# A list-scheduled decoder step: other prices for DMA loads in the planner, another lift for attention

## The chip, the cores and the metric

The kernel runs on one core of a Trainium2 chip. What counts is the device time of one execution in microseconds; of the kernel before, three runs gave a median of 1370.7 us (1368.8 to 1371.14). The engines are TensorE (PE, its weight loads PEld), VectorE (DVE), ScalarE (ACT), GpSimd (POOL) and SyncE (SP), which issues all DMAs here.

## The reference

Two layers of a hybrid decoder are applied to a prompt of 512 tokens and to 8 decoding sequences of 4 tokens, 544 columns in all, with a model width of 1024. In each layer:

```
mod = silu(c) @ w_mod + b_mod                  # 6 x 1024 columns: shift, scale, gate, twice
h = rmsnorm(x) * (1 + sc1) + sh1
z = h @ w_in                                   # q, k, v | u (SSM) | a, g (convolution)
o_attn = windowed attention with rope and sinks (8 q heads, 2 kv heads, window 128)
o_ssm  = S5 diagonal state space on u, gelu, sigmoid gate
o_conv = GLU(a, g) -> causal depthwise conv, width 31 -> LayerNorm -> silu
x = x + g1 * (concat(o_attn, o_ssm, o_conv) @ w_out)
h2 = rmsnorm(x) * (1 + sc2) + sh2
x = x + g2 * ((silu(h2 @ w_gate) * (h2 @ w_up)) @ w_down)     # inner width 2816
```

and a final RMSNorm follows. Keys, values, SSM states and convolution history are returned too.

## The kernel before, in words

**Work and tiles.** Activations lie transposed: 128 channels in the partitions, 544 tokens in two halves of 272. Each large product is split in three: weights and activations are each written as a high and a low part (hi, lo in a type of TensorE's fast path), and `mm3` multiplies hi by hi, hi by lo and lo by hi. `split` (line 543) loads a 128 x 1024 weight block of 512 KB into a tile raw, of which there are two (NRAW, line 39), writes its hi part on ScalarE or VectorE and its lo part on POOL or VectorE; of hi and lo there are four each (NW). `prefetch` (line 552) asks for blocks two ahead of their use. `mtiles` (line 567) issues the stream of matmuls.

**Modulation.** `mod_group` (line 582) computes columns of mod: per block of w_mod a load into raw (the same two buffers) and 8 matmuls of 128 x 256 into the PSUM tile mod. After the start, three groups of layer 0 (one of layer 1) run up to and in its mixing stage; the layer's last group and, in layer 0, four of the next layer run between the feed-forward matmuls (`mod_turn`, line 1399).

**The middle of a layer.** STEPS (line 206) lists in program order the projections (columns by COLS: q, v, u for the SSM, a and g for the convolution), `s5`, `attention` (line 1196), `convolve` (line 1165) for two halves of the channels, and the convolution's norm. The SSM and the convolution rearrange their data by a store to DRAM and a gather from it (tiles d_s).

**What sets the order.** Nothing in that program order is final. The program is traced once into a list of operations; `_schedule` (line 212) plans them, and the plan alone decides each engine's order, the buffer of each tile and, where two engines can do an operation, the engine. It is a list schedule: it walks through a modelled time, and whenever an engine is free it takes, among the operations whose inputs the model believes ready, the one with the highest rank. A rank is the longest modelled path to the end of the program (line 294), plus a lift (line 297) that the code sets by hand: `order.lift` is ULIFT = 150e3 in the SSM, CLIFT = 0 in the convolution, QLIFT in attention, LIFT = 150e3 or MLIFT = 700e3 for modulation blocks, in nanoseconds of rank.

Durations of operations come from `_cost`. A DMA is modelled in three parts. It begins 1100 ns after its issue or when the modelled bus is free (line 414); it holds the bus for its bytes over a rate (`lat`, line 232); and its consumer may start a hop later (`hop`, line 284), which for a DMA is one number for any consumer. `lat` and `hop` also enter the ranks. On the chip each engine runs its own list strictly in order and waits by semaphores: an operation planned too early holds up all behind it on its engine.

Of the kernel before, what the change touches and what calls it, by code (L numbers as in the profile page):

```python
# [136 lines left out]
def _box(ap):  # L137
    dims = [tuple(d) for d in ap.ap]
    pitch = max(dims[0][0], 1)
    p0, f0 = divmod(ap.offset, pitch)  # L140
    return p0, p0 + dims[0][1], f0, f0 + 1 + sum(s * (n - 1) for s, n in dims[1:])
# [58 lines left out]
FLIFT = 20e3  # L200
MT0, MT1 = 0, 1
MODS = (2, 3, 4), (4,), (1, 0, 2, 3)
PLIFT, ULIFT, CLIFT, QLIFT = (0.0, 0.0), 150e3, 0.0, 50e3
COLS = (("a0", "g0", "u0", "u1", "q4", "v0", "q0", "q1", "q2", "q3", "a1", "g1"),
        ("u0", "u1", "q4", "a0", "g0", "v0", "q0", "q1", "q2", "q3", "a1", "g1"))
STEPS = (((0, 1, 2), "taps", (3,), "c0", (4,), (5,), (6,), (7,), (8,), (9,), "s5", "attn", (10, 11), "c1", "norm"),
# [5 lines left out]
def _schedule(order, tags):  # L212
# [10 lines left out]
    lat = [0.0] * N  # L223
# [4 lines left out]
    for i, (opt, outs, ins, _, st, _, gl) in enumerate(ops):  # L228
        eng, fn = opt[0]
        if fn == "dma_start":  # L230
            a = max(outs[0], ins[0], key=lambda v: v.size() if v.space != bass.MemoryType.DRAM else 0)
            lat[i] = outs[0].size() * 4 / 360.0
        for kind, aps in ((0, ins), (1, outs)):
            for ap in aps:
                name = ap.tensor.name
                if ap.space == bass.MemoryType.DRAM and name not in tags:
                    continue
                if name in tags:
                    uses.setdefault(name, set()).add(i)
                    if name not in first:  # L240
                        first[name] = i
                box = _box(ap) if ap.space != bass.MemoryType.DRAM else (0, 1, 0, 1)
                h = hist.setdefault(name, [])
                keep = []
                for e in h:
                    b, w, j = e
                    hit = b[0] < box[1] and box[0] < b[1] and b[2] < box[3] and box[2] < b[3]
                    if hit and (w or kind) and j != i:
                        dep[i].add(j)
                    inside = kind and box[0] <= b[0] and b[1] <= box[1] and box[2] <= b[2] and b[3] <= box[3]  # L250
                    if not (inside and j != i):
                        keep.append(e)
                keep.append((box, kind, i))
                hist[name] = keep
        if eng == "PE":
            j = banks.get(outs[0].tensor.name)
            if j is not None:
                dep[i].add(j)
            banks[outs[0].tensor.name] = i
        if st:  # L260
            if last_stream is not None:
                follow[last_stream] = i
            last_stream = i
        if gl is not None:
            runs.setdefault(gl, []).append(i)
# [18 lines left out]
    def hop(j, i):  # L284
        a, b = ops[j][0][0], ops[i][0][0]
        if a[1] == "dma_start":
            return 960.0
        if a[0] == b[0]:
            return 0.0 if a[0] == "PE" else 127.0
        return 280.0 if b[0] == "PE" else 197.0 if "PE" in a or b[0] == "Pool" else 147.0  # L290

    rank = [0.0] * N
    for i in range(N - 1, -1, -1):
        rank[i] = cost[i][0] + lat[i] + max((hop(i, s) + rank[s] for s in succ[i]), default=0.0)
        if i in follow:
            rank[i] = max(rank[i], cost[i][0] + rank[follow[i]])
# [36 lines left out]
    while done < N:  # L333
        progress = True
        while progress:
            progress = False
            for e in engs:
# [28 lines left out]
                _, r, i, p = best  # L366
# [61 lines left out]
        while ev and ev[0][0] <= now:  # L428
            t, i, kind, *more = heapq.heappop(ev)
            if kind == 0:  # L430
                for o, _ in ops[i][0]:
                    bisect.insort(pool[o], (-rank[i], i))
            elif kind == 3:
                n, j = more[0]
                free[tags[n][0]].append(held[n])
                freed_by[tags[n][0], held[n]] = j
            elif kind == 1:
                for n in touch[i]:
                    left[n] -= 1
                    if left[n] == 0:  # L440
                        serial += 1
                        heapq.heappush(ev, (now + 200.0, serial, 3, (n, i)))
                for s in succ[i]:
                    if t + hop(i, s) >= arrive[s]:
                        arrive[s] = t + hop(i, s)
                        last_dep[s] = i
                    wait[s] -= 1
                    if wait[s] == 0:
                        heapq.heappush(ev, (max(arrive[s], now), s, 0))
# [1217 lines left out]
def _ordered(program):  # L1667

    trace = _Order()
    try:  # L1670
        program(trace)
    except _Traced:
        pass
    return program(_Order(_schedule(trace, trace.tiles)))
# [19 lines left out]
```

## Time and profile before

| | |
|---|---|
| median of 3 runs | 1370.7 us |
| the profiled execution | 1367.83 us, of it 1365.6 us from the first to the last instruction |
| TensorE busy | 1304.9 us (96%), 10440 matmuls |
| VectorE, ScalarE, POOL busy | 728.3, 435.0, 360.0 us |
| mean granted TensorE clock | 0.978 |
| read from HBM | 164.22 MB |

The stages of the profiled execution: up to about 45 us the start (x, modulation and SSM parameters), then layer 0's mixing to about 240, its output projection and feed-forward part to about 715, layer 1's mixing to about 905, and its feed-forward part to the end. All compute instructions are recorded under line 111, that of the helper, so that tiles and stretches tell them apart, not lines. A busy TensorE says only that a matmul was in it; the granted clock beside it says at which of two speeds (1.2 and 2.4 GHz, written as 0.5 and 1.0).

### The profile page before, as it was taken

Reading aid. Unit: us, or ns where it says so; the run is one execution under the profiler, and the core shown is the slowest. Engines: PE = TensorE matmul, PEld = TensorE weight load, DVE = VectorE, ACT = ScalarE, POOL = GpSimd, SP = SyncE. Lnnn points to the kernel's source line nnn. Section 1 sums busy time; section 2 is a strip of 40 time slices with the busy share of each in tenths; the row PEclk is TensorE's granted clock in tenths of the full one; section 3 lists DMA queues with packets and bytes.
Section 4 is the critical chain, followed back from the end, with each engine's and each line's share of the span. In section 5 each row is a group of like instructions: output and inputs, shape, how many; then the busy total and the mean of one; then the engine's idle time right before and its main releaser. Section 6 shows DMA issues by size and latency. Waiting matters only on the chain.

```text
span 1365.6 us, 25552 instructions
## 1 busy us (share of the span) xinstructions
PE 1304.9 (96%) x10440; PEld 1221.9 (89%) x10440; DVE 728.3 (53%) x1695; ACT 435.0 (32%) x929; POOL 360.0 (26%) x439
## 2 busy tenths in 40 slices
PE   7999799999999999999999999998999999999997
PEld 6987658998898888999999976898999999999997
DVE  6867975766743323334448977377534433433443
ACT  4452472442221112222226455134322211222232
POOL 7763110354422001222102521112122200222211
PEclk9999899999999999999998999999999999999998
DMA  9656474315545545222223384323352222222321
GB/s 334 214 161 197 130 252 127 117 59 174 170 142 170 171 133 166 85 93 93 94 83 98 116 261 129 120 71 105 109 154 84 83 97 94 78 78 93 97 75 66
DMA packets 79653, 176.57 MB, mean 129 GB/s; under 512 B 22768, under 2 KB 40496, under 8 KB 79536
## 3 DMA queue, kind: packets, MB, share of 16 engines
q1 hardware_dynamic: 79536, 174.94, 39.9%
q8 instruction: 82, 1.34, 0.4%
q14 instruction: 35, 0.29, 0.1%
HBM read 164.22 MB, written 10.70 MB: 128 GB/s over the span
## 4 chain that ended last, share of the span: by engine, by line
PE 64%; DMA 12%; DVE 6%; ACT 2%; issue 1%; POOL 1%; SPq 0%; DVEq 0%; ACTq 0%; POOLq 0%
PE ps_s L111 61%; DMA raw_s<-w_mod 7%; DVE pg_s L111 4%; PE mod_s L111 2%; DMA raw_s<-w_up 2%; ACT hi_s L111 1%; POOL lo_s L111 1%; DMA pg_s<-d_s 1%; DVE lo_s L111 1%; DMA raw_s<-w_down 1%; DMA d_s<-pg_s 1%; DMA raw_s<-w_gate 1%; DVE cr_s L111 1%; ACT pg_s L111 0%; DVE cs_s L111 0%
## 5 line engine op out<-in xcount | busy, mean ns | idle before, releaser
L111 PE MATMUL ps_s<-pg_s,hi_s 128*128 128x272 f32 x5504 | 1060.0, 291 | 4.5 <-ACT pg_s L111 2.6
L111 PEld LDWEIGHTS ps_s<-pg_s,hi_s 128*128 128x128 f32 x5504 | 870.1, 189 | 25.6 <-issue 16.9
L111 PE MATMUL ps_s<-pg_s,lo_s 128*128 128x272 f32 x2752 | 794.3, 290 | 0.4 <-POOL lo_s L111 0.3
L111 PEld LDWEIGHTS ps_s<-pg_s,lo_s 128*128 128x128 f32 x2752 | 519.9, 189 | 10.3 <-issue 9.2
L111 POOL TENSOR_TENSOR lo_s<-raw_s,hi_s 128x1024 fp32r<-128x1024 f32 x74 | 212.1, 2869 | 572.4 <-DVE hi_s L111 418.7
L111 ACT ACTIVATE hi_s<-raw_s 128x1024 fp32r<-128x1024 f32 x129 | 136.4, 1060 | 371.1 <-PE ps_s L111 278.1
L111 DVE TENSOR_TENSOR lo_s<-raw_s,hi_s 128x1024 fp32r<-128x1024 f32 x98 | 123.1, 1256 | 85.1 <-ACT hi_s L111 84.3
L111 PE MATMUL ps_s<-pg_s,pg_s 128*128 128x104 f32 (+10 forms) x864 | 131.6, 331 | 12.0 <-DVE pg_s L111 4.8
L111 DVE TENSOR_TENSOR pg_s<-w_s,pg_s 128x272 fp32r<-128x272 f32 x143 | 112.4, 791 | 43.0 <-ACT pg_s L111 42.6
L111 PEld LDWEIGHTS ps_s<-pg_s,pg_s 128*128 128x128 f32 (+4 forms) x864 | 105.3, 195 | 33.4 <-issue 13.4
L111 ACT ACTIVATE w_s<-ps_s 128x272 f32<-128x272 f32 (+1 forms) x172 | 66.9, 389 | 177.9 <-PE ps_s L111 173.3
L111 DVE CAST hi_s<-raw_s 128x1024 fp32r<-128x1024 f32 x43 | 29.8, 693 | 149.0 <-PE ps_s L111 145.8
L111 DVE SCALAR_TENSOR_TENSOR x<-ps_s,modT_s,x 128x272 f32<-128x272 f32 (+1 forms) x96 | 45.7, 481 | 106.0 <-PE ps_s L111 105.9
L111 ACT ACTIVATE pg_s<-w_s 128x272 fp32r<-128x272 f32 x147 | 61.5, 427 | 88.8 <-DVE w_s L111 85.3
L111 DVE TENSOR_TENSOR w_s<-w_s,ps_s 128x272 f32<-128x272 f32 x88 | 38.1, 433 | 85.7 <-ACT w_s L111 75.6
L111 PE MATMUL mod_s<-raw_s,silu_c 128*32 128x256 f32 x640 | 51.0, 394 | 22.1 <-DMA raw_s<-w_mod 20.9
L111 POOL TENSOR_TENSOR acc_s<-acc_s,w_s 128x272 f32<-128x272 f32 x9 | 9.5, 1059 | 192.3 <-ACT w_s L111 140.8
L111 ACT ACTIVATE pg_s<-ps_s 128x512 f32<-128x512 f32 (+11 forms) x100 | 34.4, 378 | 50.2 <-PE ps_s L111 44.7
L111 ACT ACTIVATE w_s<-x 128x272 f32<-128x272 f32 x70 | 29.0, 426 | 63.1 <-DVE x L111 58.7
L111 PEld LDWEIGHTS mod_s<-raw_s,silu_c 128*32 128x32 f32 x640 | 13.0, 108 | 38.5 <-DMA raw_s<-w_mod 28.1
L111 DVE TENSOR_TENSOR acc_s<-acc_s,w_s 128x272 f32<-128x272 f32 x60 | 35.4, 605 | 20.6 <-ACT w_s L111 20.5
L111 ACT ACTIVATE w_s<-w_s,modT_s,gain_s 128x272 f32<-128x272 f32 (+1 forms) x64 | 35.8, 591 | 18.7 <-DVE w_s L111 15.5
(140 smaller groups left out, 787.9 us busy)
## 6 DMA issues: line engine op xcount, KB each, us to landing
raw_s<-w_mod SPq DMA_DIRECT2D x80, 512.0 KB, 3.8
raw_s<-w_gate SPq DMA_DIRECT2D x44, 512.0 KB, 3.5
raw_s<-w_up SPq DMA_DIRECT2D x44, 512.0 KB, 3.9
raw_s<-w_down SPq DMA_DIRECT2D x44, 512.0 KB, 3.5
raw_s<-w_in SPq DMA_DIRECT2D x24, 512.0 KB, 4.7
pg_s<-cwt SPq DMA_DIRECT2D x20, 512.0 KB, 6.7
pg_s<-w_mod SPq DMA_DIRECT2D x32, 256.0 KB, 6.0
raw_s<-w_out SPq DMA_DIRECT2D x16, 512.0 KB, 3.5
```

Source lines behind the costliest of these rows:

```text
L111: r = real(*a, **k)
```

## The change

The rate in `lat` goes from 360 to 320 bytes per nanosecond; the hop behind a DMA goes from 960 to 1500 ns, with separate names for a consumer on TensorE and elsewhere, both 1500; attention's lift goes from 50e3 to 100e3. The set of operations, their shapes and the DMAs stay; the plan, and with it each engine's order, buffers and choices, is made anew.

```diff
-PLIFT, ULIFT, CLIFT, QLIFT = (0.0, 0.0), 150e3, 0.0, 50e3
+DRATE, DHOP, DPE = 320.0, 1500.0, 1500.0
+PLIFT, ULIFT, CLIFT, QLIFT = (0.0, 0.0), 150e3, 0.0, 100e3
...
         if fn == "dma_start":
             a = max(outs[0], ins[0], key=lambda v: v.size() if v.space != bass.MemoryType.DRAM else 0)
-            lat[i] = outs[0].size() * 4 / 360.0
+            lat[i] = outs[0].size() * 4 / DRATE
...
         a, b = ops[j][0][0], ops[i][0][0]
         if a[1] == "dma_start":
-            return 960.0
+            return DPE if b[0] == "PE" else DHOP
```

## Rows read from the trace of the kernel before

**Rows 1.** The page's first part: busy time, share of the span, instructions.
```profile
PE 1304.9 (96%) x10440; PEld 1221.9 (89%) x10440; DVE 728.3 (53%) x1695; ACT 435.0 (32%) x929; POOL 360.0 (26%) x439
```

**Rows 2.** TensorE's waits, whole span: us in total, times, longest.
```profile
PE mod_s L111 <- DMA raw_s<-w_mod: 20.9, 29, 2.5
PE ps_s L111 <- ACT pg_s L111: 8.2, 5, 2.9
PE ps_s L111 <- DVE pg_s L111: 6.7, 6, 3.5
...
PE ps_s L111 <- DMA pg_s<-d_s: 1.4, 2, 0.8
```

**Rows 3.** The same in 100:140, then 280:380 (two rows), 380:530 and 945:1010.
```profile
PE mod_s L111 <- DMA raw_s<-w_mod: 2.9, 2, 1.6
...
PE mod_s L111 <- DMA raw_s<-w_mod: 3.8, 8, 0.7
PE ps_s L111 <- POOL lo_s L111: 0.3, 1, 0.3
...
PE mod_s L111 <- DMA raw_s<-w_mod: 4.5, 8, 1.0
...
PE mod_s L111 <- DMA raw_s<-w_mod: 1.7, 5, 0.6
```

**Rows 4.** DMA issues (KB each, median us to landing), then all landings of raw.
```profile
raw_s<-w_mod SPq DMA_DIRECT2D x80, 512.0 KB, 3.8
...
DMA to landing us min/median/max: 3.3/3.8/9.8
```

**Rows 5.** Chain of waits, feed-forward of layer 0: start us, us, what.
```profile
331.25 4.22 DMA raw_s<-w_mod
...
335.52 0.68 PE mod_s L111 x8
...
343.33 4.67 DMA raw_s<-w_mod
...
348.04 0.68 PE mod_s L111 x8
```

**Rows 6.** TensorE in order of time around 120 us; in brackets idle before.
```profile
118.97 0.64 PE L111 MATMUL mod_s<-raw_s,silu_c 128*32 128x256 f32 x8 [1.56 <-DMA raw_s<-w_mod]
...
124.94 0.64 PE L111 MATMUL mod_s<-raw_s,silu_c 128*32 128x256 f32 x8 [1.38 <-DMA raw_s<-w_mod]
```

**Rows 7.** TensorE and ScalarE in order of time, before each feed-forward part.
```profile
272.74 0.73 ACT L111 ACTIVATE pg_s<-w_s 128x272 fp32r<-128x272 f32 x2
273.56 0.68 PE L111 MATMUL mod_s<-raw_s,silu_c 128*32 128x256 f32 x8 [2.55 <-DMA raw_s<-w_mod]
...
943.40 1.08 PE L111 MATMUL mod_s<-raw_s,silu_c 128*32 128x256 f32 x8 [2.42 <-DMA raw_s<-w_mod]
944.28 0.73 ACT L111 ACTIVATE pg_s<-w_s 128x272 fp32r<-128x272 f32 x2
```

**Rows 8.** Windows: length, busy us by engine, PEclk, DMA share, GB/s.
```profile
270.00:280.00 10.00, 7.45 (x43) 6.83 (x42) 8.87 (x32) 8.53 (x18) 4.08 (x6) 0.70 0.49 157
940.00:950.00 10.00, 7.44 (x39) 6.53 (x40) 8.57 (x20) 7.22 (x18) 3.27 (x2) 0.66 0.46 158
```

**Rows 9.** The same view of the start; PE busy is the second number.
```profile
10.00:40.00 30.00, 26.42 (x353) 20.40 (x351) 22.87 (x100) 16.62 (x37) 22.80 (x66) 1.00 1.08 369
```

**Rows 10.** Windows and TensorE's longest wait in layer 0's mixing stage (140:175, 140:210).
```profile
140.00:175.00 35.00, 27.08 (x196) 20.83 (x197) 31.68 (x117) 19.13 (x57) 6.85 (x8) 0.85 0.44 132
...
PE ps_s L111 <- DVE pg_s L111: 3.5, 1, 3.5
```

**Rows 11.** SP in order of time, end of layer 1's mixing; issues with landing.
```profile
862.37 0.38 SPq L111 DMA_DIRECT2D d_s<-pg_s  x1
...
866.70 0.33 SPq L111 DMA_DIRECT2D pg_s<-d_s  x1
...
pg_s<-d_s SPq DMA_DIRECT2D x4, 432.0 KB, 5.2
```

## Prediction

> **What bounds the kernel now.** I read the page first: TensorE is busy for 1304.9 of 1365.6 us, and the instructions are the same afterwards, so only the 60.7 us without a matmul and the stretches at the lower clock can be won [rows 1]. TensorE's waits come next: the largest entry, 20.9 us in 29 waits, is the modulation product (tile mod) standing for its load of w_mod into raw; waits for VectorE and ScalarE results (8.2, 6.7 and smaller ones) are spread over the layer's middle [rows 2]. Then the same view by stretch: 3.8 + 4.5 + 1.7 = 10.0 us of the 20.9, in 21 waits of about half a microsecond, lie in the feed-forward stretches 280 to 530 and 945 to 1010 us, and 2.9 us in 100 to 140 [rows 3]. The rest is two waits of 2.55 and 2.42 us [rows 7] and four of 0.75 us on average (20.9 - 10.0 - 2.9 - 5.0 = 3.0, 29 - 21 - 2 - 2 = 4).
>
> **Why they wait, and the load's price.** TensorE runs its list in order. The planner puts the product of a w_mod block (LIFT or MLIFT, ahead of nearly all else) where it believes the block arrives. It prices a 512 KB load (524288 bytes) at 1100 ns to start, 524288/360 = 1456 ns on the bus and 960 ns to the consumer: 3.52 us. After the change it is 1100 + 524288/320 + 1500 = 1100 + 1638 + 1500 = 4.24 us, 0.72 us more, and 0.18 us more for each further load that the planned bus has ahead of it. The trace has 3.8 us to landing in the median for w_mod, 3.3 at least and 9.8 at most over all raw loads [rows 4]; from issue to matmul, in the chain of waits, 331.25 to 335.52 is 4.27 us and 343.33 to 348.04 is 4.71 [rows 5]. The old price is 0.75 and 1.19 us short there, the new one 0.03 and 0.47.
>
> The Trainium skill (DMA: Bandwidth & Descriptors, section Anatomy of one DMA — SWDGE (gpsimd) path) puts a DMA issued by GpSimd (here SP issues) at about 2.0 us plus its bytes at 436 GB/s, an estimate of 3.2 us for such a load; by it 3.52 was dear already and dearer prices win nothing, the first rival's result. The trace disagrees: 3.2 lies under even the shortest landing, 3.3 [rows 4].
>
> **The change part by part.** All durations are of the profiled execution: 1365.6 us of span, 1367.8 us of its own time, 2.9 us under the median of 1370.7.
>
> *Feed-forward stretches.* A wait shorter than 0.72 us ends if the product merely moves back 0.72 us behind matmuls that are ready. Most of the 21 waits are (the longest are 0.7, 1.0 and 0.6 by stretch, the mean is 10.0/21 = 0.48), and what stands behind them is ready: in 280 to 380 us the feed-forward matmuls themselves wait only 0.3 us [rows 3]. So up to 9.7 of 10.0 us go. What is late next is raw itself: two buffers serve weights and w_mod, and the chain there goes load, ScalarE, VectorE or POOL, next load, and the next w_mod load of the chain goes out at 343.33, 12.1 us after the one at 331.25 [rows 5]. A matmul standing for weights then replaces some. Bounds: 0 (all waits change their name) and -10.0; I take -8.0, near the upper end on the strength of that 0.3 us.
>
> *100 to 140 us.* Two waits of 1.56 and 1.38 us [rows 6]; they are longer than 0.72, so I take 2 x 0.72 = -1.4 (bounds 0, -2.9).
>
> *The four waits in the mixing stage*, 3.0 us: next to them TensorE also stands for VectorE and ScalarE, so I take half, -1.5 (bounds 0, -3.0).
>
> *The two long waits.* At 273.56 TensorE stood 2.55 us for w_mod, but the first feed-forward matmul behind it reads an activation tile that ScalarE began to write at 272.74 and that takes half of 0.73 us; at 943.40 ScalarE began it at 944.28, later than the load [rows 7]. The load hides a bridge that stays: norm, scale, split. Of 5.0 us I take -0.5 (bounds 0 and -1). The granted clock has a mean of 0.70 and 0.66 over the ten microseconds around these idle spells [rows 8], which is 1.2 GHz for 10 x 2 x 0.30 = 6.0 and 10 x 2 x 0.34 = 6.8 us and costs half of that; since the idle stays, so does this.
>
> *Start.* From 10 to 40 us the queues move 369 GB/s [rows 9]. A plan at 320 believes a 30 us burst lasts 30 x (369/320 - 1) = 4.6 us longer than it does, and may put other work before the first projections, on VectorE and ScalarE, which run in order too. Bounds 0 and +4.6; I take +1.0, since TensorE is already busy for 26.4 of those 30 us [rows 9].
>
> The skill (same page, section Where 436 GB/s comes from) gives about 358 GB/s for one core's HBM traffic; it agrees with the row within 3% and speaks for the old 360 and against 320 at the start alone: by 358 the plan would be late by 30 x (358/320 - 1) = 3.6 us, an estimate.
>
> *Stores and gathers through DRAM* get the same dearer prices. TensorE itself waits only 1.4 us for a gather [rows 2]; I count nothing, bounds -1.4 and +1. SP's own queue is reordered by ranks that all rise alike, also nothing.
>
> *Attention's lift, 50 to 100 us of rank.* It reorders attention against what has no lift: rope, the last projections (a1, g1), the convolution, its norm, weight splits; the SSM (150) and the w_mod products (150, 700) stay above it. In 140 to 175 us VectorE is busy 31.7 of 35 us and TensorE 27.1 [rows 10]; there the SSM, still ranked higher, fills VectorE, so little moves. Attention's chains are short and limited by VectorE and ScalarE, and the planner still fills TensorE's holes with anything ready. I take 0; bounds -3.5 (TensorE's longest wait for VectorE in that stage [rows 10]) and the +12.4 worked out below.
>
> Sum: -8.0 - 1.4 - 1.5 - 0.5 + 1.0 = -10.4, so 1357.4 us for an execution like the profiled one and 1370.7 - 10.4 = 1360.3 for the median: 1360 us.
>
> **The rivals.**
>
> *The waits change their name (1369).* With two raw buffers a load is issued only when one is free; if TensorE gains 8 us it asks for weights 8 us sooner, and stands for split weights (lo) instead. For it: the loads in the chain of [rows 5], which follow each other without a rest. Against it: the 0.3 us for split weights in 280 to 380 [rows 3]. Price: only the start of the sum's small terms is left, about -2: 1369.
>
> *Slower: attention pushes the convolution out (1374).* The place is the end of layer 1's mixing. There the gated product of a1/g1 goes to DRAM at 862.37 and is gathered from 866.70 on; a gather of this size lands in 5.2 us in the median, and only then the convolution's second half and the norm can run [rows 11]. Store and gather take 4.3 + 5.2 = 9.5 us, now hidden by TensorE's other work (the output projection covers the norm after it). If attention, 50 us higher, keeps a1/g1 back by some 9 us, nothing is left to hide them: 9 us idle and a clock fall as in [rows 8], 3.4 us: +12.4. With the start's whole +4.6 in place of +1.0 (3.6 more) and half of the feed-forward gain missing (4), the sum is -10.4 + 12.4 = +2.0 at least and +9.6 at most; about 1374. It decides from X of 7 us on, where -10.4 + 7 + 3.4 is 0. Against it: TensorE's holes in attention are still filled with whatever is ready, and a1/g1 is.
>
> *The bridges close too (1350).* If the reordered VectorE and ScalarE feed the two long waits and the SSM's stretch sooner, two clock falls (3.4 us each) and some 4 us of waits go as well: -10.4 - 10 = -20, 1350. For it: the clock falls right where TensorE idles [rows 8]. Against it: nothing in the change reprices VectorE or ScalarE.
>
> **How the numbers follow.** Forecast 0.45 (its own range 1355 to 1366), more 0.20, same waits under other names 0.15, slower 0.20. What differs by 0.2% (2.7 us) can be told from no change. Faster: all of the first two, little of the third, 0.66; within: most of the third and a part of the fourth, 0.15; slower 0.19. The range reaches from a little under the 1350 case to the 1374 case: 1346 to 1375.
>
> **What would show it.** Right: TensorE's waits for raw fall from 20.9 to about 9, the 21 short ones nearly vanish, the two long ones keep their idle time under that or another name, and no new wait for lo appears. Wrong: lo or hi takes over in 280 to 530 us; a new idle spell of over 5 us with a clock fall at the end of a mixing stage; TensorE's first projections starting later; or a change of more than 5 us in TensorE's waits for VectorE and ScalarE, which would make the lift the cause, not the loads.

## The result, and the profile after

The changed kernel takes 1347.95 us in the median of 4 runs (1346.98 to 1350.76) against 1370.74 of the kernel before: a ratio of 0.984, 95% interval 0.9822 to 0.9858, or -22.8 us. The forecast was 1360.0, so the direction was right and the gain more than twice the forecast's. The profiled execution of after took 1348.77 us, 1347.0 of it span: 19.1 us less than that of before. The other 3.7 us are the distance of the two profiled executions to their medians (before 2.9 under, after 0.8 over).

The busy line of after, which answers to [rows 1], and TensorE's waits over the span (us in total, times, longest), which answer to [rows 2]:

```profile
PE 1301.1 (97%) x10440; PEld 1219.1 (91%) x10440; DVE 737.2 (55%) x1698; ACT 436.0 (32%) x928; POOL 343.0 (25%) x433
```

```profile
PE ps_s L111 <- DVE pg_s L111: 10.5, 12, 2.6
PE ps_s L111 <- ACT pg_s L111: 6.9, 5, 2.5
PE mod_s L111 <- DMA raw_s<-w_mod: 5.3, 6, 2.4
...
PE ps_s L111 <- DMA pg_s<-d_s: 0.9, 1, 0.9
```

Time without a matmul falls from 60.7 to 45.9 us. The wait for raw has gone from 20.9 us in 29 waits to 5.3 in 6; that for VectorE's pg has grown by 3.8.

The windows view by stage says where. A stage ends with the last of its stream of products (split weights by activations: the 960th ends layer 0's output projection, the 4128th its feed-forward part, the 5088th layer 1's output projection, the 8256th its feed-forward part). Columns: window, length, busy time of PE, PEld, DVE, ACT, POOL with counts, granted clock, DMA share, GB/s. First before, then after:

```profile
0.00:270.30 270.30, 244.96 (x2062) 211.85 (x2063) 192.07 (x557) 121.79 (x291) 108.78 (x204) 0.97 0.59 192
270.30:717.00 446.70, 435.49 (x3525) 411.59 (x3525) 201.06 (x435) 106.88 (x188) 106.48 (x152) 0.99 0.40 126
717.00:939.10 222.10, 211.98 (x1576) 191.55 (x1574) 159.16 (x399) 97.92 (x251) 59.17 (x52) 0.95 0.41 131
939.10:1353.90 414.80, 409.65 (x3268) 404.34 (x3267) 172.44 (x295) 106.98 (x196) 84.24 (x31) 0.99 0.29 92
```

```profile
0.00:265.70 265.70, 246.56 (x2062) 213.41 (x2063) 197.77 (x563) 115.52 (x286) 109.08 (x199) 0.96 0.61 195
265.70:701.30 435.60, 433.54 (x3524) 410.31 (x3525) 207.38 (x428) 110.66 (x190) 105.97 (x156) 1.00 0.40 129
701.30:923.40 222.10, 210.42 (x1576) 189.97 (x1573) 157.76 (x401) 100.05 (x253) 48.65 (x49) 0.95 0.41 131
923.40:1334.80 411.40, 407.78 (x3267) 402.88 (x3267) 170.66 (x295) 108.33 (x197) 77.96 (x29) 1.00 0.28 92
```

The two feed-forward parts lose 11.1 and 3.4 us, together 14.5 (861.5 to 847.0): 10.7 us of idle time (length less PE busy: 11.21 + 5.15 to 2.06 + 3.62) and 3.8 us of busy time. Layer 0 up to its output projection loses 4.6, layer 1's mixing nothing, and the end takes 0.5 longer.

At the two long waits [rows 7] and in the windows around them [rows 8], after shows (start us, us, engine, work, and in brackets the idle time before it and what ended it):

```profile
268.00 0.73 ACT L111 ACTIVATE pg_s<-w_s 128x272 fp32r<-128x272 f32 x2
268.46 0.77 PE L111 MATMUL ps_s<-pg_s,hi_s 128*128 128x272 f32 x3 [2.06 <-ACT pg_s L111]
...
927.60 1.08 PE L111 MATMUL mod_s<-raw_s,silu_c 128*32 128x256 f32 x8 [2.40 <-DMA raw_s<-w_mod]
```

```profile
265.00:275.00 10.00, 7.94 (x54) 6.69 (x53) 9.43 (x31) 8.48 (x18) 5.49 (x11) 0.83 0.46 161
925.00:935.00 10.00, 7.34 (x52) 6.37 (x51) 8.24 (x17) 7.29 (x17) 2.72 (x2) 0.83 0.45 154
```

The bridge stays, at 268.46 under ScalarE's name as forecast, but the low clock around it is shorter: a mean of 0.83 in place of 0.70 and 0.66. The first projection product, which I expected later, starts at 24.77 us, not 28.04 (what that is worth in time comes with the account of the prediction); the first row is before's, the second after's:

```profile
28.04 0.64 PE L111 MATMUL ps_s<-pg_s,hi_s 128*128 128x272 f32 x3
```

```profile
24.77 0.39 PE L111 MATMUL ps_s<-pg_s,hi_s 128*128 128x272 f32 x1
```

### The profile page after: what moved, and what is told of

Same layout as the page of the kernel before. It is cut to its first block, busy times and chain, and to the rows that moved or that the text cites. A ratio compares the mean times of both kernels' runs of the same rounds, so it can differ in the third digit from the quotient of the medians.

```text
span 1347.0 us, 25565 instructions
## 1 busy us (share of the span) xinstructions
PE 1301.1 (97%) x10440; PEld 1219.1 (91%) x10440; DVE 737.2 (55%) x1698; ACT 436.0 (32%) x928; POOL 343.0 (25%) x433
## 4 chain that ended last, share of the span: by engine, by line
PE 82%; DVE 8%; DMA 6%; ACT 2%; issue 1%; SPq 0%; POOL 0%; DVEq 0%; ACTq 0%
PE ps_s L111 79%; DVE pg_s L111 6%; PE mod_s L111 3%; DMA raw_s<-w_mod 2%; DMA d_s<-pg_s 2%; ACT pg_s L111 1%; DMA pg_s<-d_s 1%; DMA pg_s<-w_mod 1%; DMA raw_s<-w_in 1%; DVE cr_s L111 1%; DVE rs_s L111 0%; DVE cs_s L111 0%; ACT w_s L111 0%; DMA x<-xT 0%; DVE x L111 0%
## 5 line engine op out<-in xcount | busy, mean ns | idle before, releaser
L111 POOL TENSOR_TENSOR lo_s<-raw_s,hi_s 128x1024 fp32r<-128x1024 f32 x72 | 203.9, 2836 | 630.5 <-ACT hi_s L111 316.8
L111 ACT ACTIVATE hi_s<-raw_s 128x1024 fp32r<-128x1024 f32 x137 | 144.8, 1059 | 319.8 <-PE ps_s L111 243.7
L111 PE MATMUL ps_s<-pg_s,pg_s 128*128 128x104 f32 (+9 forms) x864 | 125.5, 325 | 11.8 <-DVE pg_s L111 5.6
L111 PEld LDWEIGHTS ps_s<-pg_s,pg_s 128*128 128x128 f32 (+3 forms) x864 | 98.6, 188 | 33.0 <-issue 14.8
L111 DVE TENSOR_TENSOR pg_s<-w_s,pg_s 128x272 fp32r<-128x272 f32 x147 | 104.4, 717 | 39.2 <-ACT pg_s L111 38.4
L111 DVE CAST hi_s<-raw_s 128x1024 fp32r<-128x1024 f32 x35 | 24.3, 694 | 124.7 <-PE ps_s L111 117.9
L111 DVE TENSOR_TENSOR acc_s<-acc_s,w_s 128x272 f32<-128x272 f32 x61 | 32.5, 549 | 18.6 <-ACT w_s L111 18.5
L111 DVE TENSOR_TENSOR pg_s<-pg_s,pg_s 128x256 f32<-128x256 f32 (+4 forms) x68 | 41.0, 653 | 1.3 <-ACT pg_s L111 1.1
```

Of the source, the lines that this page charges most:

```text
L111: r = real(*a, **k)
```

## The experiments

One table first, since they share its columns: the planned price of a w_mod load up to its matmul (1100 ns, bytes over rate, hop); attention's lift; when the 576th product (the last projection, usually of a1 and g1) of layer 0 ends; the end of layer 0's output projection; the two feed-forward parts together; layer 1's mixing; and the ratio to before, timed on the same chip. Stages are of the profiled executions. The expectations, printed as they were recorded, call the rate "pace", the hop "latency", and TensorE's stand behind an early convolution a "jam".

```
kernel              price lift 576th  L0 end   FF   L1 mix  median   ratio [95%]
before               3.52   50  131.4  270.3  861.5  222.1  1370.74
after                4.24  100  122.1  265.7  847.0  222.1  1347.95  0.984  [0.9822, 0.9858]
price_only           4.24   50  206.0  287.7  850.8  224.5  1378.6   1.0066 [1.0047, 1.0085]
lift_only            3.52  100  218.0  296.3  864.3  222.6  1400.22  1.0213 [1.0194, 1.0233]
hop_only             4.06   50  126.6  269.4  853.0  222.5  1360.12  0.9934 [0.9912, 0.9955]
margin520            3.52   50  155.3  274.5  866.3  224.8  1379.16  1.0064 [1.0049, 1.0079]
lift75               4.24   75  119.4  266.7  851.0  226.5  1354.85  0.989  [0.9855, 0.9924]
hop_lift100          4.06  100  133.5  269.5  853.8  228.2  1360.15  0.9922 [0.9895, 0.9949]
rate_lift100         3.70  100  133.2  265.7  858.5  215.0  1356.3   0.9885 [0.9851, 0.9919]
a1g1_first           4.24   50  153.9  282.7  849.0  222.3  1367.31  0.9974 [0.9951, 0.9997]
after_again          4.24  100  120.1  264.4  847.4  221.5  1347.87  0.9842 [0.9811, 0.9874]
after_margin510      4.24  100  147.2  271.8  849.1  225.3  1365.97  0.9962 [0.9945, 0.9978]
pe1750               4.49  100  129.5  267.7  851.0  223.0  1351.9   0.9857 [0.9831, 0.9882]
margin480_lift105    4.24  105  126.4  256.3  849.8  225.0  1340.82  0.9781 [0.9755, 0.9807]
bias_first           4.24   50  151.6  277.9  850.0  221.4  1363.97  0.9937 [0.9917, 0.9958]
pe_hop_only          4.06   50  123.0  268.3  853.2  217.3  1358.15  0.9898 [0.9871, 0.9926]
```

**The change in halves, and a placebo.** price_only has the new prices and the old lift:

```diff
-PLIFT, ULIFT, CLIFT, QLIFT = (0.0, 0.0), 150e3, 0.0, 100e3
+PLIFT, ULIFT, CLIFT, QLIFT = (0.0, 0.0), 150e3, 0.0, 50e3
```

> The three DMA prices of the change (320, 1500, 1500), attention's lift left at 50. Theory A (the prices make the whole gain): 1347 to 1352 us, TensorE's waits for raw at 5 to 8 us in place of 20.9. Theory B (the lift made what is beyond the forecast's -10): 1357 to 1363, raw waits as in A. Theory C (any new plan moves the time by up to 10 us either way, and the gain holds some of that luck): anything from 1345 to 1365, with waits for VectorE and ScalarE unlike those of the changed kernel.

lift_only has the old prices (360, 960, 960) and the new lift:

```diff
-DRATE, DHOP, DPE = 320.0, 1500.0, 1500.0
+DRATE, DHOP, DPE = 360.0, 960.0, 960.0
```

> Attention's lift at 100, the DMA prices as before. A: 1367 to 1374, raw waits still about 20 us. B: 1358 to 1362, raw waits about 20 us, less waiting in the two mixing stages. C: 1360 to 1380, not foreseeable.

margin520 is the kernel before with an unrelated constant moved:

```diff
-MARGIN, LIFT, MLIFT, WINDOW = 500.0, 150000.0, 700000.0, 4096 / 1.2
+MARGIN, LIFT, MLIFT, WINDOW = 520.0, 150000.0, 700000.0, 4096 / 1.2
```

> Prices and lift as before; only the planner's margin for choosing between VectorE and POOL goes from 500 to 520 ns, a change without a purpose that gives another order in some 6500 lines of TensorE's list. A and B: within 5 us of 1370.7, raw waits 18 to 23 us. C: more than 5 us off in either direction.

hop_only is before with 1500 ns for both hops, rate and lift as they were.

> Both hops behind a DMA at 1500 ns, the rate left at 360 and the lift at 50. A: the hop is 0.54 of the 0.72 us, so most of the raw waits go (to 5 to 9 us) and the time is 1350 to 1358. B: 1357 to 1364. C: as for the first kernel.

Neither A nor B holds: the prices alone cost 9.0 us against the before run beside them (1369.56), the lift alone 30.7, and both together gain 22.8. The hops alone gain 9.4 (1360.12, in B's range, 2 us above A's). The placebo costs 9.6, as much as the prices: that is C's point, though price_only and lift_only came out slower than its ranges too. The stages part them. The feed-forward follows the prices, not the lift or the margin: 850.8 and 853.0 with dearer loads, 864.3 and 866.3 without. What price_only loses, it loses in layer 0, 22.0 us against after. Its rows there in order of time and by windows, then after's:

```profile
102.74 7.84 PE L111 MATMUL ps_s<-pg_s,pg_s 128*128 128x104 f32 x68 [1.14 <-DVE pg_s L111]
116.20 0.79 PE L111 MATMUL ps_s<-pg_s,hi_s 128*128 128x272 f32 x2 [5.62 <-DVE pg_s L111]
...
250.95 1.05 PE L111 MATMUL ps_s<-pg_s,hi_s 128*128 128x272 f32 x3 [6.24 <-DVE pg_s L111]
```

```profile
100.00:128.00 28.00, 21.25 (x159) 20.94 (x159) 26.21 (x73) 9.50 (x23) 16.71 (x25) 0.88 0.18 56
245.00:260.00 15.00, 8.92 (x44) 8.28 (x45) 6.73 (x13) 5.76 (x10) 0.94 (x2) 0.66 0.27 76
```

```profile
121.95 1.93 PE L111 MATMUL ps_s<-pg_s,pg_s 128*128 128x104 f32 x16
124.38 1.36 PE L111 MATMUL ps_s<-pg_s,pg_s 128*128 128x104 f32 x10
...
132.18 8.45 PE L111 MATMUL ps_s<-pg_s,pg_s 128*128 128x104 f32 x64
143.22 3.96 PE L111 MATMUL ps_s<-pg_s,pg_s 128*128 128x136 f32 x16 [2.58 <-DVE pg_s L111]
```

```profile
100.00:128.00 28.00, 26.99 (x234) 22.95 (x233) 21.99 (x66) 6.04 (x15) 9.35 (x19) 1.00 0.63 191
```

The 128x104 matmuls are the convolution. In after they come when all 576 projection products of layer 0 are done. In price_only they come after 384 of them; TensorE then stands 5.62 us, a1 and g1 come only around attention (576th product at 206.0), the convolution's second half after that, and its norm is left bare in the output projection: 6.24 us idle at a clock of 0.66. That is my slower rival, late a1 and g1, in layer 0 in place of layer 1. lift_only has it too, with two stalls, and margin520 has the first stall without late a1 and g1; first lift_only, then margin520:

```profile
110.32 7.42 PE L111 MATMUL ps_s<-pg_s,pg_s 128*128 128x104 f32 x44 [4.69 <-DVE pg_s L111]
123.63 0.79 PE L111 MATMUL ps_s<-pg_s,hi_s 128*128 128x272 f32 x2 [5.89 <-DVE pg_s L111]
```

```profile
109.25 0.79 PE L111 MATMUL ps_s<-pg_s,hi_s 128*128 128x272 f32 x2 [4.55 <-DVE pg_s L111]
```

So a new theory S: the price makes the feed-forward's gain; layer 0's order is a switch that small changes can throw.

**Is it a switch?** lift75 is after with the lift at 75e3.

> The new prices with attention's lift at 75 us, halfway between 50 (1378.6 us) and 100 (1347.95). Theory S (a switch in layer 0's mixing: either TensorE's list has all 576 products of the projections before the first convolution product of layer 0, or it stops at 384 for it): this list has all 576 first, as that of after, so the whole gain is there: 1347 to 1353 us, feed-forward stretches 845 to 850 us, no idle spell of over 4 us before 200 us. Theory G (the lift itself is worth something per us of rank): about halfway, 1360 to 1367 us.

1354.85 us, 23.8 less than with 50 and 6.9 more than with 100 (on another chip; the intervals of the ratios touch). Layer 0 ends at 266.7, and no idle spell before 200 us is over 4 us: a switch, as S says, though the time lies 2 us and the feed-forward 1 us above S's ranges; the feed-forward took 851.0 and layer 1's mixing 4.4 us longer than in after.

hop_lift100 is after with the rate at 360, rate_lift100 after with both hops at 960:

```diff
-DRATE, DHOP, DPE = 320.0, 1500.0, 1500.0
+DRATE, DHOP, DPE = 360.0, 1500.0, 1500.0
```

> The new latency of 1500 ns and the lift of 100, but the old pace of 360. Its list too has all 576 projection products ahead of the convolution. Theory S: no jam, and latency alone holds most of the feed-forward gain (with lift 50 it was -8.5 of -14.3 us): 1352 to 1360 us, raw waits about 9 us. Theory P (the pace of 320 is what makes the rest): 1360 us as with lift 50, the lift adding nothing. A loss of over 5 us against before would fell both.

> The new pace of 320 and the lift of 100, but the old latency of 960 ns: a load of 512 KB is priced 0.18 us dearer than before, not 0.72. Theory S with my pricing argument (a wait goes when the price reaches the measured 4.3 us): no jam in layer 0 (all 576 projection products come first), but the feed-forward keeps most of its waits, raw waits 14 to 20 us, feed-forward 856 to 862 us, time 1358 to 1368 us. Theory P (the pace is what counts, since it adds up over loads in a row): feed-forward 848 to 852 us and 1350 to 1355 us.

hop_lift100 came out at 1360.15, on the edge of both theories: feed-forward 853.8 with raw waits of 8.1 us, as S says, but layer 1's mixing 6.1 us longer than before (its profiled execution, 1365.5 us, is the longest of its 8 runs). rate_lift100 has the feed-forward that S expects (858.5, raw 17.5) and a time 2 us under its range, because layer 1's mixing fell to 215.0. Its feed-forward rows, to set beside those of before:

```profile
265.70:710.30 444.60, 434.40 (x3524) 409.99 (x3525) 208.12 (x429) 106.92 (x189) 116.82 (x156) 1.00 0.42 127
...
925.30:1339.20 413.90, 409.78 (x3268) 404.63 (x3267) 171.51 (x295) 107.73 (x196) 81.50 (x30) 0.99 0.29 92
```

pe_hop_only is before with the dearer hop for matmuls alone (360, 960, 1500, lift 50):

> Of the whole change only the latency from a load to a matmul, 960 to 1500 ns; pace 360, latency to the other engines 960 and lift 50 as before. The w_mod load is priced at 4.06 us for its matmul, as in hop_only. Theory S (the feed-forward gain hangs on the price that the matmul sees): feed-forward 852 to 856 us (hop_only 853.0), raw waits 8 to 11 us; the list has all projections first, so no stall before 140 us, 1357 to 1364 us. If the weights' loads, whose consumers are ScalarE, VectorE and POOL, need the dearer price too: 858 to 862 us and 1364 to 1370.

853.2 us of feed-forward, hop_only's 853.0: only the price that the matmul sees counts there. pe1750 is after with that hop at 1750:

> The changed kernel with the latency to a matmul at 1750 ns in place of 1500, so that a load is priced at 4.49 us, between the two measured 4.27 and 4.71. The list has all 576 projection products first. Theory S: the feed-forward's short waits are already gone in after, so a dearer price takes at most the rest (raw 5.3 us to 3 or less) and the feed-forward stays at 846 to 851 us; 1346 to 1353 us. If the price is still too low, feed-forward under 844 us and 1342 to 1346. If a dearer price only delays the products, over 1355.

851.0: no further gain. By price the feed-forward takes 861.5 to 866.3 (3.52 us), 858.5 (3.70), 853.0 to 853.8 (4.06), 847.0 to 851.0 (4.24) and 851.0 (4.49), whatever the lift, the margin and layer 0's order. Its idle time alone is 16.4 to 18.9 us, 14.3, 7.3 to 8.9, 5.7 to 8.2 and 7.0. The fall between 3.70 and 4.06 is clear; the other steps are no larger than the 4 to 5 us by which plans of one price differ.

The order itself can be counted in the traces. In ten runs, before and after among them, at least 146 of the 160 matmuls of layer 0's convolution (128x104) come behind the 576th product; layer 0 ends at 256.3 to 270.3 us. In the other six, 80 of them come at the 384th: it ends at 271.8 to 282.7 in the four where the 576th product ends by 155.3, and at 287.7 and 296.3 where it ends at 206.0 and 218.0. So before and after are on the same side of the switch, and margin520 and after_margin510 threw it by the margin alone.

**What makes layer 0's loss.** a1g1_first is price_only with the last projections of layer 0 raised:

```diff
             else:
+                order.lift = 200e3 if l == 0 and step == (10, 11) else 0.0
                 project(step)
+                order.lift = 0.0
```

> The new prices with the old lift of 50, and besides the projections a1 and g1 of layer 0 raised by 200 us, so that their 576th product no longer comes after attention; the list still has the convolution's first half at product 384. Theory S in its first form (two costs in price_only: the stall at 116 us, and the late a1 and g1 with the norm bridge of 6.2 us and 10.2 us at half the clock behind them, worth 6.2 + 5.1 = 11.3): the second goes, the first stays: 1364 to 1370 us, the long idle spell at 251 us gone, the one at 116 us still there. If the stall alone makes the loss, it stays at 1377 to 1380; if the late a1 and g1 alone make it, 1348 to 1354.

1367.31 us, 11.3 less than price_only, the sum that was expected. The 6.24 us are gone (TensorE stands 2.86 there), and the first stall is still there, if shorter. By stage it is less clear: layer 0 ends only 5.0 us sooner, the rest of the 8.8 us between the two spans being spread over the later stages. Its stall:

```profile
113.32 0.49 PE L111 MATMUL ps_s<-pg_s,hi_s 128*128 128x272 f32 x2 [3.35 <-DVE pg_s L111]
```

bias_first is price_only with the bias adds that empty the convolution's PSUM banks (tiles ps) raised above the SSM, for the first half of layer 0's channels:

```diff
                 cb = pa_[:, A_CB + i * 8 + g0:A_CB + i * 8 + g0 + 4]
+                order.lift = 1000e3 if l == 0 and i == 0 else CLIFT
...
+                order.lift = CLIFT
```

> price_only (new prices, lift 50) with one thing raised: VectorE's two bias adds behind each half of layer 0's first convolution, which free the PSUM banks that TensorE waits for at 116 us (5.62 us). Theory S with its cause (the banks are held because the SSM, ranked 150 us higher, keeps VectorE from the bias adds): the stall shrinks to under 2.5 us, a1 and g1 come before attention, no idle spell over 4 us at the norm, 1358 to 1368 us; feed-forward unchanged at 848 to 852 us. If the stall only goes along with the bad order and does not cause it: 1375 to 1381 us.

1363.97 us, inside S's range, and the stall shrank to 0.81. The rows bear out what holds TensorE up. In price_only the convolution ends at 110.58 (102.74 + 7.84). VectorE does the adds that empty its banks between other work, at 112.20, 114.79 and 115.87, and TensorE goes on at 116.20, just behind the third. In margin520, a1g1_first, after_margin510 and lift_only's second stall, too, such a 128x32 add out of a PSUM tile is what ended the wait. In bias_first VectorE stands 4.16 us for the convolution and does the adds as it ends:

```profile
112.20 0.41 DVE L111 TENSOR_TENSOR pg_s<-ps_s,par 128x256 f32<-128x256 f32 x1
...
114.79 0.41 DVE L111 TENSOR_TENSOR pg_s<-ps_s,par 128x256 f32<-128x256 f32 x1
...
115.87 0.18 DVE L111 TENSOR_TENSOR pg_s<-ps_s,par 128x32 f32<-128x32 f32 x1
```

```profile
114.63 0.85 DVE L111 TENSOR_TENSOR pg_s<-ps_s,par 128x256 f32<-128x256 f32 x3 [4.16 <-PE ps_s L111]
```

But little is won at this place. In bias_first the same 68 matmuls take 10.91 us, at a mean granted clock of 0.70 in place of 1.00, and TensorE is back at the projections at 115.63, only 0.57 us sooner than in price_only:

```profile
103.91 10.91 PE L111 MATMUL ps_s<-pg_s,pg_s 128*128 128x104 f32 x68 [0.90 <-DVE pg_s L111]
115.63 0.49 PE L111 MATMUL ps_s<-pg_s,hi_s 128*128 128x272 f32 x2 [0.81 <-DVE pg_s L111]
```

```profile
103.91:114.82 10.91, 10.91 (x68) 10.74 (x68) 6.18 (x18) 7.77 (x20) 7.47 (x17) 0.70 0.39 134
```

What the two runs have in common is that a1 and g1 come some 52 to 54 us earlier (153.9 and 151.6 in place of 206.0). With that layer 0 ends 5.0 and 9.8 us sooner, and the medians fall by 11.3 and 14.6. That late a1 and g1 are a part of the loss is shown by a1g1_first, which moves nothing else by hand and loses the long idle spell at the norm; in bias_first they come earlier along with the adds, so its gain cannot be put down to the stall. Both still end layer 0 later than the changed kernel, by 17.0 and 12.2 us (in bias_first 6.4 of idle and 5.8 of busy time). These belong to the early convolution as a whole (stall, low clock, later projections), which these runs do not part further. Nor was the switch traced to one decision of the planner.

**The changed kernel's own luck.** after_again is after itself, after_margin510 after with MARGIN at 510:

> The changed kernel itself once more, so that the three beside it stand against it on one chip, and to see how far its stages move from one profiled execution to the next. Expected 1347 to 1351 us, ratio 0.984, feed-forward stretches 846 to 850 us, layer 0 to the end of its output projection 264 to 268 us.

> The changed kernel with an unrelated constant moved by 2% (the planner's margin for giving work to a second engine, 500 to 510 ns). Its list has the jam again: it stops at 384 projection products for the convolution. Theory S (the price makes the feed-forward gain, layer 0's order makes or loses the rest, whatever flips it): feed-forward 847 to 852 us as in after, layer 0 late at 276 to 288 us, 1358 to 1372 us. Theory L (the lift's value in after is that of attention itself, not of the jam): lift and prices are those of after, so 1347 to 1353 us.

after_again: 1347.87 us, the length of each of these stages within 1.3 us of the first profile's. after_margin510: 1365.97 us in the median (its profiled execution, 1359.8, is the shortest of its 12 runs), with the feed-forward at 849.1 and the stall back, though layer 0 ends at 271.8, before the 276 that I had expected at least:

```profile
101.18 6.95 PE L111 MATMUL ps_s<-pg_s,pg_s 128*128 128x104 f32 x60 [0.67 <-DVE pg_s L111]
111.85 0.49 PE L111 MATMUL ps_s<-pg_s,hi_s 128*128 128x272 f32 x2 [3.72 <-DVE pg_s L111]
```

So 2% of an unrelated constant takes back 18.1 us of the 24.3 that after gains on that chip and leaves the feed-forward's gain alone; theory L, that the lift is worth something by itself, falls.

**A faster version.** margin480_lift105 has both moved the other way.

> A try at a faster version: the changed kernel with the lift at 105 us and the margin at 480 ns. All 576 projection products come first, and layer 0's convolution is finished some 9 us earlier in the list's own times than in after. Expected 1339 to 1348 us; feed-forward as after (846 to 850 us), layer 0's end 258 to 264 us. If the order in layer 0 past the projections does not matter, 1347 to 1351.

1340.82 us against after's 1347.87 on the same chip, from layer 0 alone, which ends 8.1 us before after_again's (at 256.3, 2 us sooner than expected); the feed-forward and layer 1's mixing take 2.4 and 3.5 us longer. Its first stage:

```profile
0.00:256.30 256.30, 242.42 (x2062) 209.67 (x2063) 200.02 (x565) 114.98 (x285) 110.29 (x198) 0.99 0.64 202
```

## Why the prediction was half right

**Feed-forward, right mechanism, mis-sized: -8.5 taken, -14.5 measured.** The short waits were counted at -8.0 of 10.0, with a matmul standing for weights in place of some; in after TensorE has no wait at all between 280 and 530 us, and only the long one and 0.3 us behind it between 925 and 1000, so all 10.0 went [rows 3]. The two long waits fell from 4.97 to 2.06 + 2.40 = 4.46 us: the -0.5 taken. Together the idle time fell by 10.7 in place of 8.5. The step that failed here is "since the idle stays, so does this" for the low clock: idle stayed, but the feed-forward's busy time fell by 3.8 us, and the clock in the two windows makes 3.0 of them (10 x 0.13 + 10 x 0.17). The runs show that this part is no property of the change. Behind the same idle of 2.06 us for the same matmul, the window's clock is 0.83 in both profiles of after and 0.69 and 0.66 in lift75 and hop_only:

```profile
266.00:276.00 10.00, 7.94 (x45) 6.69 (x44) 8.98 (x30) 8.47 (x18) 4.04 (x6) 0.69 0.53 166
```

```profile
270.00:280.00 10.00, 7.94 (x42) 7.14 (x42) 9.30 (x34) 7.74 (x18) 5.71 (x12) 0.66 0.46 153
```

That the price was short of the measured 4.27 and 4.71 [rows 5] is borne out by the row of prices: 3.70 left 14.3 of the 16.4 us of idle time, 4.06 about half, 4.24 down to 5.7, and 4.49 took no more. By the rule of the Trainium skill that I set against it (DMA: Bandwidth & Descriptors, section Anatomy of one DMA — SWDGE (gpsimd) path; 3.2 us for such a load, an estimate) 3.52 would have been dear enough; the feed-forward's 8 to 14 us disagree.

**Start: +1.0 taken, about 0 measured.** I had the plan's slower bus delay the first projections. The first product starts 3.3 us sooner instead (28.04 to 24.77), but that is order, not time: by 40 us TensorE has begun 380 matmuls, 390 before. In those 40 us it idles 1.3 us less, and its mean clock is 0.96 in place of 1.00, which takes 1.6 us back. Before's row, then after's, then after's answer to [rows 9]:

```profile
0.00:40.00 40.00, 32.98 (x390) 26.96 (x390) 25.32 (x111) 20.07 (x43) 30.51 (x87) 1.00 1.01 340
```

```profile
0.00:40.00 40.00, 34.24 (x380) 28.41 (x381) 26.70 (x110) 18.96 (x42) 33.39 (x88) 0.96 1.01 332
...
10.00:40.00 30.00, 27.61 (x349) 21.78 (x348) 22.73 (x94) 14.30 (x32) 25.90 (x68) 0.94 1.08 362
```

The Trainium skill's 358 GB/s (same page, section Where 436 GB/s comes from) again agrees with the row (362), but the 3.6 us of delay that I derived from it do not appear.

**100 to 140 us and the four mixing waits: -1.4 and -1.5 taken.** The first fell from 2.9 to 1.0 us, -1.9; the others from 3.0 to 5.3 - 2.4 - 1.0 = 1.9, -1.1. Together -3.0 for the -2.9 taken. Layer 0's idle time fell by 6.2 us (25.3 to 19.1, from the windows) and its busy time rose by 1.6, which makes the 4.6 by which it ends sooner. Of the 6.2, 1.3 lie before 40 us, 1.9 in 100 to 140, and 3.0 in 60 to 100, where I had forecast nothing: before stands there for ScalarE, after does not stand at all. No run shows which part of the change did that. Before's rows, then after's:

```profile
60.00:100.00 40.00, 36.95 (x282) 36.10 (x282) 31.03 (x60) 19.82 (x42) 25.78 (x32) 0.91 0.59 170
...
88.54 1.11 PE L111 MATMUL ps_s<-cst,pg_s 128*128 128x128 f32 x4 [2.89 <-ACT pg_s L111]
```

```profile
60.00:100.00 40.00, 40.00 (x314) 39.80 (x313) 34.19 (x68) 21.53 (x43) 30.40 (x43) 0.96 0.59 178
```

**Attention's lift: 0 taken; this step failed.** The prediction added the prices' terms (-10.4) and the lift's (0) as if each held by itself. Neither does: the prices alone made +9.0, the lift alone +30.7, and the lift beside the new prices -30.7 (1378.6 to 1347.95, on two chips). "TensorE's holes in attention are still filled with whatever is ready, and a1/g1 is" failed: in price_only and lift_only a1 and g1 came 75 and 87 us later than in before. Both lose mainly by the switch in layer 0 (its end at 287.7 and 296.3 in place of 270.3), which neither before nor after throws. The sign that I had set for the lift, a change of more than 5 us in the waits for VectorE and ScalarE, did not appear in after (+3.2 and -1.5 over all tiles), and yet the lift decides beside these prices. I took the term as small because its parts were; a list schedule does not add up that way, and the bounds of -3.5 to +12.4 were too near on both sides. That the change as a whole gained is in this part luck: with MARGIN at 510 it is worth -6.2 us.

**The sum.** For the profiled executions -19.1 against -10.4: of the missing 8.7 the feed-forward makes 6.0. The rest of the span makes 2.2 (start, mixing and end: -4.1 measured, -1.9 taken), and 0.5 lies outside the spans. The rival that closes two bridges as well named the right time (1350) for a wrong reason: both bridges stayed.

## What to carry to other kernels

A list scheduler's price for a load must reach from issue to consumer as the trace measures it; here a price 0.75 to 1.19 us short was paid in 29 waits, 20.9 us, on an engine that runs its list in order. Judge such a change stage by stage, against a placebo that moves an unrelated constant: here the feed-forward gained 8 to 14 us in every plan with a price of 4.06 us or more, while layer 0's end moved between 256.3 and 296.3, by the margin alone as by the prices and the lift. Before timing a new plan, look in its list for work that a late stage needs and that has slid back, as a1 and g1 here.

## What was not expected of the hardware

Nearly the same idle spell before the same matmul (2.06 us, in a1g1_first 2.08) was followed by a low clock of different length from one kernel to the next: over ten microseconds a mean of 0.83 in after, 0.69 and 0.66 in lift75 and hop_only, and no fall at all in a1g1_first. In all four TensorE had been busy without a break, at a clock of 1.00, for the ten microseconds before. The difference between 1.00 and 0.66 is 3.4 us of full clock.

```profile
285.45 0.78 PE L111 MATMUL ps_s<-pg_s,hi_s 128*128 128x272 f32 x4 [2.08 <-ACT pg_s L111]
...
282.00:292.00 10.00, 7.55 (x59) 6.47 (x57) 9.40 (x30) 8.46 (x18) 5.49 (x11) 1.00 0.51 161
```

And in 100 to 128 us price_only and bias_first have the same mean clock, 0.88, though one idles 6.75 us there and the other 1.71:

```profile
100.00:128.00 28.00, 26.29 (x194) 25.98 (x194) 20.83 (x62) 11.74 (x29) 15.85 (x28) 0.88 0.26 88
```
